# Moving the float32 remainders of the PEER stages from GpSimd to VectorE, and pinning the row gathers

## The chip, the cores and the metric

The kernel runs on 1 core of one Trainium2 chip. The metric is the device time in microseconds of one launch; a figure is the median of several runs. A profiled execution has a time of its own, which stands beside its span in the table below.

## What is computed

The reference is a two-block network on 512 tokens of width 1024: a first block (differential attention and a mixture of 16 experts), then a second block (forgetting attention, an RWKV-7 time mix, a gated merge, a layer norm) that ends in a PEER layer. Only the PEER layer and the last layer norm matter here:

```
q = (xb @ w_q).reshape(t, 8, 2, 128)                    # 8 heads, two halves each
s = einsum('thpd,hpkd->thpk', q, sub_keys)
top_s, top_i = top_k(s, 16)                             # per half
cand = top_s[.., 0, :, None] + top_s[.., 1, None, :]    # 16 x 16 sums
best_s, best_pos = top_k(cand, 16); idx = the pair's index in 16384 experts
gate = softmax(best_s)
h = gelu(einsum('thkd,td->thk', u_table[idx], xb))
y = einsum('thk,thkd->td', gate * h, v_table[idx])
```

## The kernel before

It is one program for one core, written in a framework that traces it and then fixes, at build time, the order of the instructions in each engine's queue: among the instructions whose inputs its own cost estimates call ready, the one that was traced first goes first. On the chip each queue then runs strictly in that order. `keep_in_program_order` pins one instruction behind the instruction that was traced just before it on the same engine; nothing else is pinned by it, and instructions traced later may still be placed ahead.

Matrix products of full float32 precision are made of three passes (`mm3`, lines 47 to 51). For that each operand is split in two halves by `split` (lines 53 to 61): ScalarE writes the rounded half `hi` (line 57), and VectorE, or the engine given as `eng`, writes the remainder `lo = src - hi` (line 58). `load_split` (lines 66 to 72) puts a load on SyncE's DMA queue in front of it.

The PEER layer (`peer`, from line 1747) works on 512 tokens in 4 tiles of 128. For the first three tiles (384 tokens) it is dense: all 16384 rows of the table u are multiplied with the tokens, in 128 blocks of 128 rows, and all rows of v are summed with weights that are zero except for the chosen ones. For the last tile the chosen rows alone are gathered (`peer_rows`, lines 1714 to 1744). The stages, with their time from the start of the span:

- **Top-k stage** (about 1268 to 1537 us). For each of 8 heads, `peer_topk` (line 1625) loads and splits the two query weights of the head (line 1631), multiplies, scores, and picks the 16 best on VectorE. After each head, `spill` (line 1779) multiplies the next 3, 4 or 5 blocks of u (`u_block`, line 1769: load, split, 24 matmuls into one of two PSUM banks, Gelu on ScalarE) and stores them in DRAM (`hd`), to use TensorE while VectorE sorts: 30 blocks in all.
- **Scatter stage** (about 1537 to 1707 us). `peer_scatter` (line 1691) is called 48 times. Each call makes one-hot tiles on VectorE (lines 1699, 1700, 1704: four instructions of 128x1024 float16), multiplies them on TensorE (line 1710) and copies the result to `Gs` (line 1712), from where 6 stores bring it to DRAM. After every second call one block of u is spilled: 24 blocks. I call two calls and one block a step.
- **Main loop** (from about 1707 us; 130 turns). It first spills 6 more blocks of u (line 1826), then for each of the 128 blocks loads the stored product or makes it, multiplies with `G`, splits it, loads and splits a block of v, and multiplies into six PSUM accumulators. Among these turns the 257 steps of `peer_rows` are dealt out: 128 times a gather of a row of u for each of 128 tokens (line 1725, a DMA of 128 x 4 KB issued by GpSimd, indices in SBUF) and a dot product with the token on VectorE (line 1732, pinned); one step for the weights; 128 times a gather of v and a multiply-add on VectorE (line 1741, pinned). The gathered rows have 5 buffers.

In the top-k and the scatter stage the splits of u (line 58 by `u_block`) and all query weights but the first have `eng` set to GpSimd. In the 6 blocks after the scatter stage and in the main loop VectorE makes them. GpSimd's other work here is two small tables (lines 1797, 1802), the two loads of the layer norm's rows at the start of the main loop (line 77, called by line 1836), the gathers, and four additions at the very end (line 1558).

Of the kernel before, what the change touches and what calls it, by code (L numbers as in the profile page):

```python
# [20 lines left out]
T, D, NT, KC = 512, 1024, 4, 8  # L21
# [6 lines left out]
class Kern:  # L28
# [1596 lines left out]
    def peer_topk(self, wp, h, xT, sk, iota16, pk):  # L1625

        nc, I = self.nc, self.I
        tv = self.t(wp, [128, 2, NT, 16], F32, "tv")
        ti = self.t(wp, [128, 2, NT, 16], U32, "ti")
        for s in range(2):  # L1630
            w = self.load_split(wp, I["wq"][2 * h + s], [128, KC, 128], "w", 2, 2, nc.gpsimd if h or s else None)
            p = self.psx()
            for kc in range(KC):
                self.mm3(p, [z[:, kc, :] for z in w], [z[:, kc, :] for z in xT], kc == 0, kc == KC - 1)
            q = self.t(wp, [128, T], F32, "q")
            nc.scalar.activation(q, p, AF.Copy)
            p = self.psx([128, NT, 128])
            for t in range(NT):
                nc.tensor.matmul(p[:, t, :], q[:, t * 128:(t + 1) * 128], sk[:, 2 * h + s, :], start=True, stop=True)
            sc = self.t(wp, [128, NT, 128], F32, "sc")  # L1640
            nc.scalar.activation(sc, p, AF.Copy)
            for t in range(NT):
                self.top16(wp, sc[:, t, :], 128, tv[:, s, t, :], ti[:, s, t, :], "t")

        cand = self.t(wp, [128, NT, 80], F32, "cand")
        nc.vector.tensor_tensor(cand[:, :, 0:16], tv[:, 0, :, 0:1].to_broadcast([128, NT, 16]), tv[:, 1], OP.add)
        nc.vector.tensor_tensor(cand[:, :, 16:72].rearrange("p t (a b) -> p t a b", b=8),
                                tv[:, 0, :, 1:8, None].to_broadcast([128, NT, 7, 8]),
                                tv[:, 1, :, None, 0:8].to_broadcast([128, NT, 7, 8]), OP.add)
        nc.vector.tensor_tensor(cand[:, :, 72:80], tv[:, 0, :, 8:16], tv[:, 1, :, 0:1].to_broadcast([128, NT, 8]), OP.add)  # L1650
        bs = self.t(wp, [128, NT, 16], F32, "bs")
        bp = self.t(wp, [128, NT, 16], U32, "bp")
        for t in range(NT):
            self.top16(wp, cand[:, t], 80, bs[:, t, :], bp[:, t, :], "c")

        pf = self.t(wp, [128, 2, NT, 16], F32, "pf")
        q, r = pf[:, 0], pf[:, 1]
        ai = self.t(wp, [128, NT, 16], I32, "ai")
        ab = self.t(wp, [128, 2, NT * 16], BF, "ab")
        a, b = (ab[:, i].rearrange("p (t k) -> p t k", t=NT) for i in range(2))  # L1660
        t9 = self.t(wp, [128, NT, 16], F32, "t9")
        nc.vector.tensor_copy(r, bp)
        nc.vector.tensor_scalar(ai, r, -3.5, 1.0 / 8, OP.add, OP.mult)
        nc.vector.tensor_copy(q, ai)
        nc.vector.scalar_tensor_tensor(r, q, -8.0, r, OP.mult, OP.add)
        nc.vector.scalar_tensor_tensor(t9, q, 9.0, r, OP.is_equal, OP.mult)
        nc.vector.tensor_tensor(r, r, t9, OP.subtract)
        nc.vector.scalar_tensor_tensor(a, q, -1.0, t9, OP.add, OP.add)
        nc.vector.tensor_scalar(a, a, 0.0, None, OP.max)
        nc.vector.tensor_scalar(t9, q, 1.0, 8.0, OP.is_equal, OP.mult)  # L1670
        nc.vector.tensor_tensor(b, r, t9, OP.add)
        tf = self.t(wp, [128, 2, NT, 16], BF, "tf")
        nc.vector.tensor_copy(tf, ti)
        for s in range(2):
            eq = self.t(wp, [128, 16, NT * 16], BF, "eq")
            nc.vector.tensor_tensor(eq, iota16, ab[:, s, None, :].to_broadcast([128, 16, NT * 16]), OP.is_equal)
            e4 = eq.rearrange("p a (t k) -> p t a k", t=NT)
            nc.vector.tensor_tensor(e4, e4, tf[:, s, :, :, None].to_broadcast([128, NT, 16, 16]), OP.mult)
            for n in (8, 4, 2):
                nc.vector.tensor_tensor(eq[:, 0:n], eq[:, 0:n], eq[:, n:2 * n], OP.add)  # L1680
            e1 = [eq[:, i].rearrange("p (t k) -> p t k", t=NT) for i in range(2)]
            nc.vector.tensor_tensor(pk[:, :, s, h, :], e1[0], e1[1], OP.add)
        g = pk[:, :, 2, h, :]
        nc.vector.tensor_tensor(g, bs, bs[:, :, 0:1].to_broadcast([128, NT, 16]), OP.subtract)
        nc.scalar.activation(g, g, AF.Exp)
        zs = self.t(wp, [128, NT], F32, "zs")
        nc.vector.tensor_reduce(zs, g, AX.X, OP.add)
        nc.vector.reciprocal(zs, zs)
        nc.vector.tensor_tensor(g, g, zs[:, :, None].to_broadcast([128, NT, 16]), OP.mult)
# [24 lines left out]
    def peer_rows(self, sp, x, pk):  # L1714


        nc, I = self.nc, self.I
        t, keep = NT - 1, self.tc.keep_in_program_order
        ix = self.t(sp, [128, 8, 16], U32, "ix")
        g = self.t(sp, [128, 8, 16], F32, "rg")  # L1720
        dots = self.t(sp, [128, 8, 16], F32, "dots")

        def row(name, h, j):
            r = self.t(sp, [128, D], F32, "row", 5)
            nc.gpsimd.indirect_dma_start(r, None, I[name], bass.IndirectOffsetOnAxis(ap=ix[:, h, j:j + 1], axis=0))  # L1725
            return r

        def dot(h, j):
            if j == 0:
                nc.vector.scalar_tensor_tensor(ix[:, h], pk[:, t, 0, h], 128.0, pk[:, t, 1, h], OP.mult, OP.add)  # L1730
            r = row("u", h, j)
            keep(nc.vector.tensor_tensor_reduce(r, r, x[:, t, :], 1.0, 0.0, OP.mult, OP.add, dots[:, h, j:j + 1]))  # L1732

        def weights():
            nc.scalar.activation(g, dots, AF.Gelu)
            nc.vector.tensor_tensor(g, g, pk[:, t, 2], OP.mult)
            nc.scalar.activation(x[:, t, :], x[:, t, :], AF.Copy, scale=2.0 ** 0.25)

        def add(h, j):
            r = row("v", h, j)  # L1740
            keep(nc.vector.scalar_tensor_tensor(x[:, t, :], r, g[:, h, j:j + 1], x[:, t, :], OP.mult, OP.add))  # L1741

        picks = [(h, j) for h in range(8) for j in range(16)]
        return [lambda a=a: dot(*a) for a in picks] + [weights] + [lambda a=a: add(*a) for a in picks]


    def peer(self, x):

        nc, I, tc = self.nc, self.I, self.tc
        NB, ND = 60, NT - 1  # L1750
        TD = ND * 128
        with ExitStack() as ph:
# [26 lines left out]
            def spill(n, eng=None):  # L1779
                for b in range(self.ahead, min(self.ahead + n, NB)):  # L1780
                    a = self.t(up, [128, TD], F32, "hs", 2)
                    u_block(b, a, eng)
                    nc.sync.dma_start(hd[b], a)
                self.ahead = min(self.ahead + n, NB)
# [9 lines left out]
            with ExitStack() as sub:  # L1794
# [3 lines left out]
                with tc.tile_pool(name="ptk", bufs=2) as wp, tc.tile_pool(name="psk", bufs=1) as kp:  # L1798
                    sk = self.t(kp, [128, 16, 128], F32, "sk")
                    nc.sync.dma_start(sk, I["sk"])  # L1800
                    iota16 = self.t(kp, [128, 16, NT * 16], BF, "iota16")
                    nc.gpsimd.iota(iota16, pattern=[[1, 16], [0, NT * 16]], base=0, channel_multiplier=0, allow_small_or_imprecise_dtypes=True)
                    for h in range(8):
                        self.peer_topk(wp, h, xT, sk, iota16, pk)
                        spill(5 if h == 7 else 4 - h % 2, nc.gpsimd)
                with tc.tile_pool(name="pgs", bufs=2) as wp:
                    keys = []
                    for t in range(ND):
# [9 lines left out]
                    for t in range(ND):  # L1818
                        for i in range(2):
                            Gs = self.t(wp, [128, 128, 64], F32, "Gs")  # L1820
                            for b in range(8):
                                self.peer_scatter(wp, *keys[t], i * 8 + b, Gs, iota2)
                                if b % 2 == 1:
                                    spill(1, nc.gpsimd)
                            nc.sync.dma_start(gd[2 * t + i], Gs)
            spill(NB)
            pss.close()
# [2 lines left out]
            wp = ph.enter_context(tc.tile_pool(name="pdw", bufs=2))  # L1830
# [167 lines left out]
```

## Time and profile before

| | |
|---|---|
| Runs | 2598.91 us median of 3 (2596.53 to 2601.98) |
| Profiled execution | 2601.8 us |
| its span, first to last instruction | 2600.1 us |
| granted TensorE clock, mean | 0.967 |
| TensorE busy (matmul) | 2411.4 us, 93% |
| VectorE busy | 1997.3 us, 77% |
| ScalarE busy | 1129.0 us, 43% |
| GpSimd busy | 941.2 us, 36% |

In the rows below PE is TensorE, DVE is VectorE, ACT is ScalarE, POOL is GpSimd and SP is SyncE. A group has the line, the engine and operation, output<-inputs, shapes and count, then busy time in us and the mean of one in ns, then the idle time of the engine just before it and what ended that. L58 is line 58 of the kernel. PEclk is the clock that TensorE was granted as a share of full speed: 1.00 is the level of 2.4 GHz, 0.50 that of 1.2 GHz.

### The profile page before, as it was taken

What the parts mean: (1) busy time and instruction counts of PE and PEld (TensorE: products, weight loads), DVE (VectorE), ACT (ScalarE), POOL (GpSimd) and SP (SyncE); (2) the same over time, 40 slices, a digit from 0 to 9 for tenths busy, and PEclk for the clock granted to TensorE, in tenths of its full rate; (3) what the DMA queues carried; (4) which work ended last, traced back from release to release, by engine and by line L of the source; (5) the groups of instructions that cost most, each with busy time, mean ns of one, the idle gap of its engine ahead of it and who ended that gap; (6) DMA issues with size and microseconds to landing.
All of it is one profiled execution on the core that took longest, in us unless ns stands there. A gap on an engine that the chain in (4) does not pass through costs nothing.

```text
span 2600.1 us, 36041 instructions
## 1 busy us (share of the span) xinstructions
PE 2411.4 (93%) x13302; PEld 1987.8 (76%) x13302; DVE 1997.3 (77%) x3696; ACT 1129.0 (43%) x1660; POOL 941.2 (36%) x674
## 2 busy tenths in 40 slices
PE   6999979999799999899989988899999999999998
PEld 5666666666577787777779878898788879888886
DVE  7698678988866558647699997857788778787886
ACT  3366546777544543224334434443333333332333
POOL 2577422223311103000255456614454434444440
PEclk8999989999899999899999999999999999999999
DMA  7442359999631122115254226689899899999992
GB/s 251 131 153 97 109 198 338 366 358 364 225 110 49 64 70 76 58 58 174 100 165 140 98 78 241 251 325 350 314 352 352 304 335 330 332 324 334 334 321 81
DMA packets 229671, 566.30 MB, mean 218 GB/s; under 512 B 27794, under 2 KB 83138, under 8 KB 228596
## 3 DMA queue, kind: packets, MB, share of 16 engines
q1 hardware_dynamic: 180512, 394.88, 43.4%
q0 software_dynamic: 44176, 159.38, 17.7%
q10 hardware_dynamic: 4804, 9.72, 1.0%
q8 instruction: 105, 1.72, 0.3%
q14 instruction: 74, 0.61, 0.1%
HBM read 511.99 MB, written 51.92 MB: 217 GB/s over the span
## 4 chain that ended last, share of the span: by engine, by line
PE 19%; DVE 12%; issue 12%; POOL 7%; DMA 6%; ACT 1%; SPq 0%; POOLq 0%; DVEq 0%; ACTq 0%
POOL row L1725 5%; PE psu L51 2%; PE psu L49 2%; DMA act<-hd 2%; PE psu L50 2%; DMA row<-in_v,ix 2%; POOL u_lo L58 2%; PE py L50 2%; PE py L51 2%; PE py L49 2%; DVE x L1741 1%; DMA row<-in_u,ix 1%; DVE ohB L1704 1%; PE psb L49 1%; PE psx L1710 1%
## 5 line engine op out<-in xcount | busy, mean ns | idle before, releaser
L51 PE MATMUL psu<-x4T_hi,u_lo 128*128 128x384 f32 x1024 | 347.5, 340 | 18.5 <-POOL u_lo L58 18.5
L49 PE MATMUL psu<-x4T_hi,u_hi 128*128 128x384 f32 x1024 | 350.0, 342 | 0.5 <-ACT act L1775 0.4
L50 PE MATMUL psu<-x4T_lo,u_hi 128*128 128x384 f32 x1024 | 346.5, 338 | 0.0
L50 PE MATMUL py<-v_lo,W_hi 128*128 128x512 f32 x768 | 304.7, 397 | 15.1 <-DVE v_lo L58 15.1
L49 PE MATMUL py<-v_hi,W_hi 128*128 128x512 f32 x768 | 304.1, 396 | 10.9 <-ACT W_hi L57 7.8
L51 PE MATMUL py<-v_hi,W_lo 128*128 128x512 f32 x768 | 304.3, 396 | 1.8 <-DVE W_lo L58 1.8
L1725 POOL DMA_INDIRECT row<-in_v,ix x128 | 185.7, 1450 | 224.4 <-DVE x L1741 192.9
L1725 POOL DMA_INDIRECT row<-in_u,ix x128 | 182.9, 1429 | 228.9 <-DVE dots L1732 203.6
L58 POOL TENSOR_TENSOR u_lo<-u_raw,u_hi 128x1024 fp32r<-128x1024 f32 x54 | 193.7, 3594 | 143.7 <-ACT u_hi L57 143.7
L57 ACT ACTIVATE W_hi<-act 128x384 fp32r<-128x384 f32 x128 | 66.5, 524 | 407.3 <-DVE act L1859 407.3
L58 DVE TENSOR_TENSOR ew_lo<-ew_raw,ew_hi 128x2048 fp32r<-128x2048 f32 x93 | 216.8, 2331 | 34.1 <-ACT ew_hi L57 32.8
L57 ACT ACTIVATE u_hi<-u_raw 128x1024 fp32r<-128x1024 f32 x128 | 134.8, 1055 | 188.3 <-PE psu L50 106.8
L51 PEld LDWEIGHTS psu<-x4T_hi,u_lo 128*128 128x128 f32 x1024 | 195.1, 191 | 19.5 <-POOL u_lo L58 19.4
L49 PEld LDWEIGHTS psu<-x4T_hi,u_hi 128*128 128x128 f32 x1024 | 195.4, 191 | 4.6 <-ACT act L1775 0.8
L50 PEld LDWEIGHTS psu<-x4T_lo,u_hi 128*128 128x128 f32 x1024 | 195.2, 191 | 3.6
L57 ACT ACTIVATE w_hi<-w_raw 128x1024 fp32r<-128x1024 f32 (+1 forms) x103 | 101.8, 992 | 221.0 <-PE psb L50 99.2
L57 ACT ACTIVATE ew_hi<-ew_raw 128x2048 fp32r<-128x2048 f32 x93 | 178.2, 1916 | 42.3 <-PE psa L51 41.3
L50 PEld LDWEIGHTS py<-v_lo,W_hi 128*128 128x128 f32 x768 | 146.7, 191 | 47.9 <-DVE v_lo L58 19.9
L1732 DVE CUSTOM_DVE_ANT_0 row<-row,x 128x1024 f32<-128x1024 f32 x128 | 155.7, 1239 | 34.9 <-DMA row<-in_u,ix 34.8
L1741 DVE SCALAR_TENSOR_TENSOR x<-row,rg,x 128x1024 f32<-128x1024 f32 x128 | 164.0, 1282 | 23.5 <-DMA row<-in_v,ix 21.8
L58 DVE TENSOR_TENSOR v_lo<-v_raw,v_hi 128x1024 fp32r<-128x1024 f32 x128 | 156.3, 1221 | 31.0 <-ACT v_hi L57 30.9
L49 PEld LDWEIGHTS py<-v_hi,W_hi 128*128 128x128 f32 x768 | 146.8, 191 | 41.6 <-ACT W_hi L57 9.8
(667 smaller groups left out, 5862.1 us busy)
## 6 DMA issues: line engine op xcount, KB each, us to landing
u_raw<-in_uT SPq DMA_DIRECT2D x128, 512.0 KB
v_raw<-in_v SPq DMA_DIRECT2D x128, 512.0 KB
ew_raw<-in_wgate SPq DMA_DIRECT2D x32, 1024.0 KB
ew_raw<-in_wup SPq DMA_DIRECT2D x32, 1024.0 KB
ew_raw<-in_wdown SPq DMA_DIRECT2D x32, 1024.0 KB
gd<-Gs SPq DMA_DIRECT2D x6, 4096.0 KB
G<-gd SPq DMA_DIRECT2D x32, 768.0 KB
w_raw<-in_w2b SPq DMA_DIRECT2D x39, 512.0 KB
```

The source lines that it names most:

```text
L49: mm(out, L[0], R[0], start=start, stop=False)
L50: mm(out, L[0], R[1], start=False, stop=False)
L51: mm(out, L[1], R[0], start=False, stop=stop)
L57: nc.scalar.activation(hl[0], src, AF.Copy)
L58: (eng or nc.vector).tensor_tensor(hl[1], src, hl[0].bitcast(F32), OP.subtract)
L1704: nc.vector.tensor_tensor(B[i], oh, bc(gp[:, i]), OP.mult)
L1710: nc.tensor.matmul(p[:, u, :], A[j], B[i][j], start=i == 0, stop=i == 1)
L1725: nc.gpsimd.indirect_dma_start(r, None, I[name], bass.IndirectOffsetOnAxis(ap=ix[:, h, j:j + 1], axis=0))
L1732: keep(nc.vector.tensor_tensor_reduce(r, r, x[:, t, :], 1.0, 0.0, OP.mult, OP.add, dots[:, h, j:j + 1]))
L1741: keep(nc.vector.scalar_tensor_tensor(x[:, t, :], r, g[:, h, j:j + 1], x[:, t, :], OP.mult, OP.add))
```

## The change

The engine argument of the split goes away at three places, so that the remainders of all blocks of u and of all query weights are made by VectorE; and the gather of a row is pinned behind the instruction traced before it on GpSimd.

```diff
@@ peer_topk
-            w = self.load_split(wp, I["wq"][2 * h + s], [128, KC, 128], "w", 2, 2, nc.gpsimd if h or s else None)
+            w = self.load_split(wp, I["wq"][2 * h + s], [128, KC, 128], "w", 2, 2)
@@ peer_rows
-            nc.gpsimd.indirect_dma_start(r, None, I[name], bass.IndirectOffsetOnAxis(ap=ix[:, h, j:j + 1], axis=0))
+            keep(nc.gpsimd.indirect_dma_start(r, None, I[name], bass.IndirectOffsetOnAxis(ap=ix[:, h, j:j + 1], axis=0)))
@@ peer
-                        spill(5 if h == 7 else 4 - h % 2, nc.gpsimd)
+                        spill(5 if h == 7 else 4 - h % 2)
...
-                                    spill(1, nc.gpsimd)
+                                    spill(1)
```

The instruction traced before the first gather on GpSimd is the second of the two row loads of line 1836; before each later gather it is the gather before.

## Rows read from the trace of the kernel before

**Rows 1.** Busy time by stage: stretch, its length, PE, PEld, DVE, ACT, POOL, PEclk, DMA share, GB/s

```profile
1268.00:1537.00 269.00, 247.61 (x1300) 226.44 (x1301) 248.52 (x1057) 110.06 (x148) 132.31 (x57) 0.96 0.42 140
1353.00:1529.00 176.00, 168.34 (x897) 154.50 (x896) 172.66 (x772) 72.09 (x96) 83.64 (x33) 0.98 0.37 121
1537.00:1707.00 170.00, 148.73 (x1303) 140.87 (x1303) 140.26 (x187) 80.73 (x142) 110.01 (x21) 0.94 0.59 219
1707.00:1748.00 41.00, 40.51 (x232) 39.73 (x231) 14.25 (x16) 15.80 (x22) 1.15 (x2) 1.00 0.94 340
1748.00:2560.00 812.00, 784.19 (x3735) 685.71 (x3734) 648.48 (x825) 277.86 (x382) 359.46 (x248) 0.98 0.91 326
```

**Rows 2.** Groups by line and shape, VectorE, 1280 to 1537 us

```profile
L1676 DVE TENSOR_TENSOR eq<-iota,ab 128x1024 bf16<-128x1024 bf16 x16 | 26.3, 1646 | 0.0
...
L1680 DVE TENSOR_TENSOR eq<-eq 128x512 bf16<-128x512 bf16 x16 | 19.8, 1235 | 0.0
...
L1647 DVE TENSOR_TENSOR cand<-tv 128x224 f32<-128x224 f32 x8 | 8.9, 1119 | 0.0
...
L1732 DVE CUSTOM_DVE_ANT_0 row<-row,x 128x1024 f32<-128x1024 f32 x3 | 5.9, 1974 | 1.0 <-DMA row<-in_u,ix 1.0
```

**Rows 3.** The same lines alone: shortest/median/longest in ns, first and last start

```profile
L1647 DVE TENSOR_TENSOR cand<-tv x8: 381/384/2895, 1306.0 to 1510.3; 128x224 f32<-128x224 f32 x8
L1676 DVE TENSOR_TENSOR eq<-iota,ab x16: 678/694/2897, 1315.0 to 1523.5; 128x1024 bf16<-128x1024 bf16 x16
```

**Rows 4.** Timeline of VectorE, 1522 to 1530 us: start, duration, instruction

```profile
1524.08 0.41 DVE L1680 TENSOR_TENSOR eq<-eq 128x512 bf16<-128x512 bf16 x1
```

**Rows 5.** Groups by line and shape, GpSimd, 1268 to 1537 us

```profile
L58 POOL TENSOR_TENSOR u_lo<-u_raw,u_hi 128x1024 fp32r<-128x1024 f32 x33 | 83.7, 2541 | 84.9 <-ACT u_hi L57 84.9
L58 POOL TENSOR_TENSOR w_lo<-w_raw,w_hi 128x1024 fp32r<-128x1024 f32 x15 | 39.1, 2605 | 35.7 <-ACT w_hi L57 35.7
L1725 POOL DMA_INDIRECT row<-in_u,ix x8 | 9.1, 1132 | 5.8 <-DVE pk L1689 3.9 <-issue 1.7 <-DVE tv L1619 0.2
```

**Rows 6.** Timeline of GpSimd and of ScalarE in the top-k stage

```profile
1323.14 1.05 POOL L1725 DMA_INDIRECT row<-in_u,ix  x1 [3.93 <-DVE pk L1689]
...
1346.57 0.26 ACT L1685 ACTIVATE pk<-pk 128x64 f32<-128x64 f32 x1 [12.65 <-DVE pk L1684]
```

**Rows 7.** Waits of TensorE, 1268 to 1537 us: total, times, longest

```profile
PE psx L1639 <- ACT q L1636: 10.5, 2, 8.6
```

**Rows 8.** Busy time in stretches of 5 us (columns as in rows 1)

```profile
1345.00:1350.00 5.00, 0.00 (x0) 0.00 (x0) 4.73 (x24) 3.40 (x5) 0.35 (x1) 0.64 0.11 39
1350.00:1355.00 5.00, 3.95 (x13) 3.53 (x14) 5.00 (x3) 1.60 (x3) 5.00 (x2) 0.50 0.31 101
```

**Rows 9.** Waits of TensorE, 1537 to 1760 us

```profile
PE psu L51 <- POOL u_lo L58: 18.5, 3, 6.4
```

**Rows 10.** The chain of work that ended last, 1241 to 1760 us: start, duration, what

```profile
1544.47 14.90 POOL u_lo L58
...
1599.78 14.31 POOL u_lo L58
...
1685.52 1.86 PE psx L1710 x32
1691.60 1.86 PE psx L1710 x32
```

**Rows 11.** Timeline of VectorE: two one-hot instructions in a row; two remainders in a row

```profile
1597.95 0.68 DVE L1700 TENSOR_TENSOR ohA<-iota,pkT 128x1024 f16<-128x1024 f16 x1
1598.55 0.68 DVE L1704 TENSOR_TENSOR ohB<-oh,gp 128x1024 f16<-128x1024 f16 x1
...
1754.43 2.35 DVE L58 TENSOR_TENSOR u_lo<-u_raw,u_hi 128x1024 fp32r<-128x1024 f32 x2
```

**Rows 12.** Timeline of GpSimd at the start of the main loop

```profile
1721.62 0.59 POOL L77 DMA_DIRECT2D lng<-in_ln_g  x1 [26.07 <-DVE lneps L1838]
...
1748.34 1.74 POOL L1725 DMA_INDIRECT row<-in_u,ix  x1 [25.57 <-DVE dots L1732]
```

## The prediction

> **What bounds the kernel now.** I read the busy time by stage first. The change touches the top-k stage (269 us), the scatter stage (170 us) and the first turns of the main loop [rows 1]. In the stretch from 1353 to 1529 us VectorE is busy for 172.7 of 176 us: the top-k stage is bound by VectorE, with TensorE close behind at 168.3 [rows 1]. The scatter stage is bound by nothing steadily: TensorE 148.7 and VectorE 140.3 of 170 us, at a granted clock of 0.94 [rows 1]. The main loop belongs to TensorE (784 of 812 us), with the DMA engines at a share of 0.91 [rows 1]. So GpSimd, which the change empties, is the bound nowhere; the question is what its instructions do to the others.
>
> Next the groups of VectorE, beside the shortest and median of the same lines. A one-hot compare of line 1676 takes 694 ns in the median but 1646 in the mean, and 2897 at its longest [rows 2, 3]. The 2.2 us between median and longest are nearly one whole remainder on GpSimd (mean 2541 and 2605 ns [rows 5]). The reader is to see that VectorE stands still behind GpSimd's instruction, now and then, in the stage in which VectorE is the bound.
>
> Then the chain of work in the scatter stage: it runs through remainders of u on GpSimd that took 14.9 and 14.3 us [rows 10], and TensorE waits three times, 18.5 us in all, for such a one [rows 9]. Here it is GpSimd that stands still, behind a run of VectorE instructions that start 0.60 us apart [rows 11].
>
> Last the hoisted row work. Eight gathers and three dot products run inside the top-k stage, from 1323 us on [rows 2, 5, 6], though they are traced in the main loop. The dots hold VectorE for 5.9 us and 1.0 us of waiting for data [rows 2]; after them ScalarE, stuck at an Exp, waits 12.65 us for VectorE [rows 6], and TensorE waits 8.6 us in turn [rows 7] and restarts at half clock [rows 8].
>
> **The change part by part, the top-k stage.** It removes 48 remainders from GpSimd (33 of u, 15 of w [rows 5]) and adds 48 to VectorE. Two in a row took 2.35 us on VectorE [rows 11], 1.18 each; 48 x 1.18 = 56.6 us. Those ahead of the first head fall where VectorE has most of its 20.5 us of idle time [rows 1]; I put six there, which leaves 42 x 1.18 = 49.6 us on the bound.
>
> What VectorE gets back are its stops. Counted from mean less undisturbed time: line 1676, 16 x (1646 - 694) = 15.2 us; line 1680 of 512 columns, 16 x (1235 - 410) = 13.2 us; line 1647, 8 x (1119 - 384) = 5.9 us [rows 2, 3, 4]. That is 34.3 us that are certain. At most each of the 48 costs 2.2 us, 106 us. I take 46, nearer the counted end, since the other lines with two inputs are few or short. The dots leave this stage too: 6.9 us. Net on VectorE: +49.6 - 46 - 6.9 = **-3.3 us**; with the counted stops alone +8.4, and at the other end no more than about -20, since TensorE needs 247.6 us of the 269 as it is [rows 1]. TensorE loses its wait of 8.6 us and its slow restart, but VectorE is the later of the two, so I credit only 2 us for that: **-5 us**.
>
> The Trainium skill, page "SBUF — State Buffer", section "Who interferes with whom", says that a VectorE instruction with two SBUF inputs and a GpSimd instruction that reads SBUF exclude each other, each holding a shared port for the whole instruction. By that alone a remainder on GpSimd would lose at most one VectorE instruction, 0.7 us, and be done in about 3.3 us; the scatter stage would have no stall and the change would gain nothing there (the sum below would be near -2). The measured 14.3 us say that the loser can lose many times in a row; the rows decide.
>
> **The scatter stage.** A step (two calls and one block) takes TensorE 6.08 us where nothing stalls: the starts of the scatter matmuls of neighbouring steps are 1685.52 and 1691.60 [rows 10]. On VectorE it will need 8 x 0.60 + 1.18 = 5.98 us [rows 11], with no stop behind GpSimd. So 24 steps are 24 x 6.08 = 146 us, against 170 now: at most 24 us, of which 18.5 are the named wait and the rest its slow restarts (a mean clock of 0.94 [rows 1]). With VectorE only 2% shorter than TensorE some steps will slip; I take **-19 us**, with 0 and -24 as ends.
>
> **The gathers.** Pinned behind the load of the layer norm's rows, which is issued at 1721.6 us [rows 12], the first gather can no longer go at 1323 us [rows 6]. Five go at once after that load, three more as dots end; now the ninth gather goes at 1748.3 [rows 12]. On GpSimd that costs nothing: it is idle then. The three dots, 3 x 1.2 us, go to a stretch where VectorE is busy for 14.3 of 41 us [rows 1]. But eight gathers are 8 x 512 KB = 4.2 MB, and they leave a stage with a DMA share of 0.42 for one with 0.91 to 0.94; at 326 GB/s [rows 1] that is 12.9 us of transfers, in front of loads of u and v on which the first turns depend. The share leaves some 7% free, and TensorE has the six spilled blocks in hand; I take **+3 us**, with 0 and +13 as ends. Within the loop the order of gathers was the order of the pinned dots already; the rest of the pins I cost at nothing: a gather waits for a buffer that a dot frees, as now [rows 12]. If gathers were placed later than now, the dots would come late, and with them the loads behind VectorE; that cover is VectorE's 160 us of idle time in the loop [rows 1].
>
> **Sum:** -5 - 19 + 3 = -21 us. The profiled execution took 2601.8 us, 2.9 more than the median of 2598.9; from the median, -21 gives 2578, from the profiled one 2581. I say **2579 us**.
>
> **The rivals.**
>
> *VectorE's queue takes over the waits (slower).* On GpSimd the remainders waited 84.9 + 35.7 = 120.6 us for ScalarE's halves, and nobody stood behind them but other remainders [rows 5]. On VectorE the sort, the scores' consumers and the Exp's input stand behind them. If a third of these waits is kept, 40 us come on top of a bound engine: -21 + 40 = +19, **2618 us**. It decides from 21 us on, a little over a sixth of the waits, 2.6 us a head. For it: VectorE is full at 98% [rows 1], so any wait there is a loss, and a remainder that comes late behind a sort starves TensorE, which then restarts at half clock [rows 8]. Against it: the order is built on the readiness of inputs, GpSimd's stops that it could not foresee are gone, and in the main loop VectorE makes such remainders with TensorE busy for 784 of 812 us [rows 1].
>
> *The scatter stage stays stuck.* If VectorE, at 5.98 of 6.08 us a step, falls behind, half the gain goes: **2589 us**.
>
> *The loop pays in full for the gathers.* +13 in place of +3: **2589 us**. For it: the DMA share of 0.94 just then [rows 1].
>
> *The pin does not bind.* If the dots stay hoisted, VectorE keeps 6.9 us, the loop gets 3 back: **2583 us**.
>
> *The stops were more than counted.* At the end that TensorE sets, -20 in the top-k stage: **2564 us**.
>
> **How the numbers follow.** The forecast, 2566 to 2588, gets 0.50; the pin that does not bind 0.05; the stuck scatter stage and the full price of the gathers, 2588 to 2593, 0.11 together; more stops, 2556 to 2566, 0.08; two of the bad cases together, or a small loss in VectorE's queue, which end within 0.2% of now (2593.7 to 2604.1; about what a measurement of this kernel can tell from no change), 0.09; the slower rival 0.17. So faster 0.74, same 0.09, slower 0.17. A range from 2560 to 2606 leaves out some of the upper gain and most of the slower rival, about 0.2. The forecast's own range, of one sign, is 2566 to 2588.
>
> **What would show it.** Right: no line 58 on GpSimd; longest of lines 1676 and 1647 near their medians; the scatter stage near 150 us with no wait of TensorE for `u_lo` over 2 us, at a clock near 1.00; no gather before the layer norm's rows; the Exp's longest wait on ScalarE well under 12 us. Wrong: waits of VectorE for `u_hi` or `w_hi` in the top-k stage beyond 20 us, the stage longer than 269 us with TensorE waiting for `u_lo` from VectorE, or waits for loads of u and v in the first turns of the loop.

## The result, and the profile after

The changed kernel takes **2560.36 us** (median of 4 runs, 2556.33 to 2562.07) against 2600.44 (4 runs, 2596.53 to 2603.17) beside it: a ratio of 0.9845, 95% interval 0.9826 to 0.9863. That is 40 us faster, where 21 us were forecast. 2560.36 lies inside the stated range of 2560 to 2606 us by 0.4 us, and below the forecast's own range of 2566 to 2588.

The profiled execution has a span of 2557.9 us against 2600.1. To see where the 42.2 us went, I take for each kernel the same marks: the start of the first transpose of line 1766, the first one of line 1811, the first and the last copy of line 1712, and the first and last multiplication with G of line 1859. The lines of one view, of the changed kernel (shortest/median/longest in ns, first and last start):

```profile
L1766 PE MATMUL psx<-ident,x x32: 272/273/476, 1272.0 to 1281.7; 128*128 128x128 f32 x32
...
L1811 PE MATMUL psx<-ident,pk x9: 272/273/329, 1512.7 to 1515.2; 128*128 128x128 f32 x9
...
L1712 ACT ACTIVATE Gs<-psx x96: 589/600/624, 1521.0 to 1661.4; 128x512 f32<-128x512 f32 x96
...
L1859 DVE TENSOR_TENSOR act<-act,G x128: 546/551/562, 1707.5 to 2534.1; 128x384 f32<-128x384 f32 x128
```

The same of the kernel before:

```profile
L1766 PE MATMUL psx<-ident,x x32: 272/273/472, 1268.0 to 1279.2; 128*128 128x128 f32 x32
...
L1811 PE MATMUL psx<-ident,pk x9: 421/421/478, 1528.8 to 1530.9; 128*128 128x128 f32 x9
...
L1712 ACT ACTIVATE Gs<-psx x96: 587/598/633, 1538.1 to 1706.5; 128x512 f32<-128x512 f32 x96
...
L1859 DVE TENSOR_TENSOR act<-act,G x128: 546/552/577, 1744.8 to 2575.9; 128x384 f32<-128x384 f32 x128
```

The differences of neighbouring marks, in us, for these two and for the experiments below (their names are explained there; "ahead" is the work before the PEER layer, which no kernel here touches but e12_all_vector):

| kernel | ahead | top-k | gap | scatter | loop's start | loop | end | top-k to end |
|---|---|---|---|---|---|---|---|---|
| before | 1268.0 | 260.8 | 9.3 | 168.4 | 38.3 | 831.1 | 24.2 | 1332.1 |
| after | 1272.0 | 240.7 | 8.3 | 140.4 | 46.1 | 826.6 | 23.8 | 1285.9 |
| after_again | 1272.6 | 241.2 | 8.3 | 140.5 | 45.7 | 823.4 | 23.8 | 1282.9 |
| e1_no_pin | 1269.6 | 243.3 | 8.3 | 141.3 | 38.8 | 827.1 | 23.8 | 1282.6 |
| e2_pin_only | 1268.7 | 254.0 | 9.1 | 169.6 | 45.5 | 828.0 | 24.2 | 1330.4 |
| e3_scatter_only | 1279.2 | 254.2 | 7.7 | 140.6 | 36.8 | 825.5 | 23.8 | 1288.6 |
| e4_topk_only | 1264.2 | 250.0 | 9.6 | 169.5 | 36.6 | 828.8 | 23.9 | 1318.4 |
| e5_early_gathers | 1268.7 | 241.0 | 8.3 | 140.5 | 36.7 | 826.2 | 23.8 | 1276.5 |
| e7_idle_subtract | 1273.4 | 294.8 | 7.0 | 140.5 | 46.5 | 829.3 | 23.8 | 1341.9 |
| e8_write_only | 1271.5 | 242.8 | 8.2 | 140.5 | 46.2 | 825.4 | 23.8 | 1286.9 |
| e9_w_back | 1266.3 | 242.3 | 8.3 | 141.5 | 46.1 | 824.7 | 23.8 | 1286.7 |
| e10_u_back | 1269.1 | 250.7 | 7.6 | 140.6 | 45.9 | 827.9 | 23.8 | 1296.5 |
| e11_half_subtract | 1273.7 | 258.9 | 7.0 | 140.5 | 46.8 | 828.6 | 23.8 | 1305.6 |
| e12_all_vector | 1273.1 | 241.1 | 8.3 | 140.5 | 45.6 | 823.7 | 23.8 | 1283.0 |

So the 42.2 us are +4.0 ahead of the change (where profiles of equal code differ by up to 15 us, so this is no effect of it), **-20.1 in the top-k stage**, -1.0 in the gap, **-28.0 in the scatter stage**, **+7.8 at the loop's start**, -4.5 in the loop and -0.4 at the end. The -4.5 has no cause that is shown here: the same code gave 826.6 and 823.4 us. Stages are compared below, not spans, since the stretch ahead of them varies so much.

Busy time by stage after, to be read beside [rows 1] (columns as there):

```profile
1272.00:1512.70 240.70, 236.09 (x1264) 215.39 (x1264) 230.94 (x1074) 108.71 (x146) 0.84 (x1) 0.99 0.41 131
1353.00:1510.00 157.00, 157.00 (x850) 144.96 (x850) 155.53 (x762) 69.55 (x92) 0.00 (x0) 1.00 0.38 121
1521.00:1662.00 141.00, 139.19 (x1291) 133.83 (x1289) 139.78 (x212) 79.48 (x140) 0.00 (x0) 1.00 0.70 265
1662.00:1703.00 41.00, 36.72 (x201) 36.08 (x200) 13.30 (x15) 11.52 (x16) 11.05 (x10) 0.96 0.98 388
```

Same view, the top-k stage of before between its own marks:

```profile
1268.00:1528.80 260.80, 239.46 (x1264) 218.82 (x1264) 240.94 (x1035) 109.82 (x147) 132.31 (x57) 0.96 0.43 143
```

In the top-k stage TensorE stood idle for 260.8 - 239.5 = 21.3 us; now it is 4.6 us, and from 1353 to 1510 us it is busy without a gap at full clock. The bound has moved from VectorE to TensorE. The groups of VectorE there (1272 to 1521 us), to be read beside [rows 2]:

```profile
L58 DVE TENSOR_TENSOR u_lo<-u_raw,u_hi 128x1024 fp32r<-128x1024 f32 x32 | 38.9, 1214 | 1.0 <-ACT u_hi L57 1.0
...
L58 DVE TENSOR_TENSOR w_lo<-w_raw,w_hi 128x1024 fp32r<-128x1024 f32 x16 | 19.4, 1212 | 4.3 <-ACT w_hi L57 4.3
...
L1676 DVE TENSOR_TENSOR eq<-iota,ab 128x1024 bf16<-128x1024 bf16 x16 | 11.0, 687 | 0.0
...
L1680 DVE TENSOR_TENSOR eq<-eq 128x512 bf16<-128x512 bf16 x16 | 6.7, 416 | 0.0
...
L1647 DVE TENSOR_TENSOR cand<-tv 128x224 f32<-128x224 f32 x8 | 3.0, 378 | 0.0
```

The remainders take 1.21 us each, near the 1.18 taken from [rows 11], and the means of the other three lines have fallen to their undisturbed values; for ScalarE's halves VectorE waits 4.3 + 1.0 = 5.3 us in all. The longest of line 1676, 2897 ns in [rows 3], is now 693. Of the waits, those that answer to [rows 6, 7] are small too:

```profile
PE psx L1639 <- ACT q L1636: 1.1, 1, 1.1
...
DVE tv L1619 <- ACT sc L1641: 1.1, 1, 1.1
...
ACT pk L1685 <- DVE pk L1684: 27.3, 8, 4.1
```

Before, the first was 10.5 us, the second was 13.3 us in 4 waits, and the longest of the third was 12.65.

The chain of work that ended last, in the scatter stage, is now a train on TensorE in place of the two long remainders of [rows 10]:

```profile
1543.43 1.86 PE psx L1710 x32
...
1658.82 1.86 PE psx L1710 x32
```

From 1543.43 to 1658.82 there are 19 steps of 6.07 us in the mean, without a slip.

### The profile page after: what moved, and what is told of

Its sections match the earlier page's. It is cut to its first block, busy times and chain, and to the rows that moved or that the text cites. A ratio compares the mean times of both kernels' runs of the same rounds, so it can differ in the third digit from the quotient of the medians.

```text
span 2557.9 us, 36037 instructions
## 1 busy us (share of the span) xinstructions
PE 2396.9 (94%) x13302; PEld 1977.2 (77%) x13302; DVE 1991.3 (78%) x3765; ACT 1130.3 (44%) x1660; POOL 710.5 (28%) x605
## 4 chain that ended last, share of the span: by engine, by line
PE 18%; issue 16%; DVE 11%; POOL 8%; DMA 3%; ACT 1%; POOLq 0%; DVEq 0%; ACTq 0%
POOL row L1725 8%; PE psu L49 2%; PE psu L51 2%; PE psu L50 2%; DMA row<-in_v,ix 2%; PE psx L1710 2%; PE py L50 1%; PE py L51 1%; PE py L49 1%; DVE u_lo L58 1%; PE psb L49 1%; PE psb L50 1%; PE psb L51 1%; DVE eq L1678 1%; DVE x L1741 1%
## 5 line engine op out<-in xcount | busy, mean ns | idle before, releaser
L1732 DVE CUSTOM_DVE_ANT_0 row<-row,x 128x1024 f32<-128x1024 f32 x128 | 153.2, 1219 | 46.2 <-DMA row<-in_u,ix 46.2
L51 PEld LDWEIGHTS py<-v_hi,W_lo 128*128 128x128 f32 x768 | 146.1, 190 | 34.9 <-DVE W_lo L58 4.6
```

What stands on the lines that cost most here:

```text
L51: mm(out, L[1], R[0], start=False, stop=stop)
```

## The experiments

The theories. **Stops**: a GpSimd subtraction, which reads SBUF, holds up VectorE's next instruction for nearly its whole length; the top-k stage pays for that. **Lateness**: the stage pays because TensorE waits for remainders that GpSimd finishes late. Both could be true of different stages. A third question is what the pin of the gathers is worth.

### One part at a time (e1 to e4)

e1_no_pin is the change without the pin, e2_pin_only the pin alone:

```diff
# e1_no_pin, against after
-            keep(nc.gpsimd.indirect_dma_start(...))
+            nc.gpsimd.indirect_dma_start(...)
# e2_pin_only, against before
-            nc.gpsimd.indirect_dma_start(...)
+            keep(nc.gpsimd.indirect_dma_start(...))
```

> The change without its pin: all remainders on VectorE, gathers free to be placed early. Theory A (three separate causes: VectorE's stops behind GpSimd in the top-k stage, GpSimd's starving in the scatter stage, the hoisted dots): the dots are back in the top-k stage and cost about the 7 us that they held VectorE, the loop gets 3 back; scatter stage 141 us as with the change; in all 2564 to 2570 us, 4 to 10 above the change. Rival B (the hoisted dots are the main cause of the top-k stage's loss, by way of ScalarE's Exp and TensorE's restart): the top-k stage falls back by 12 us or more, 2572 to 2580 us.

> The pin alone: remainders stay on GpSimd. Theory A: top-k stage about 7 us shorter, scatter stage 169 us as before, loop 3 longer: about 2596 us. Rival B: top-k stage 15 us or more shorter, 2583 to 2588 us.

e3_scatter_only and e4_topk_only divide the moved remainders:

```diff
# e3_scatter_only, against before
-                                    spill(1, nc.gpsimd)
+                                    spill(1)
# e4_topk_only, against before
-            w = self.load_split(..., "w", 2, 2, nc.gpsimd if h or s else None)
+            w = self.load_split(..., "w", 2, 2)
...
-                        spill(5 if h == 7 else 4 - h % 2, nc.gpsimd)
+                        spill(5 if h == 7 else 4 - h % 2)
```

> Only the 24 blocks of the scatter stage have their remainders on VectorE. Theory A: scatter stage 169 to 141 us, all else as before: 2572 us, no longer wait of TensorE for u_lo, one-hot instructions at their median of 0.68 us throughout. Rival C (what the scatter stage gains is given back at the start of the loop, where the DMA share is 0.94): 2580 to 2590 us.

> Only the top-k stage has its remainders on VectorE; no pin. Theory A: that stage shorter by the stops less the remainders, some 12 of the 20 us that the whole change took from it (the dots keep theirs): about 2588 us; lines 1676 and 1647 at their medians throughout. Rival D (the waits for ScalarE's halves move into VectorE's queue once the dots disturb it): no gain or a loss, 2598 us or more.

Measured, as ratios to before on the same chip (2604.27 us, 23 runs): e1 0.9818 (0.9792 to 0.9844), e2 1.0008 (0.9992 to 1.0024), e3 0.9856 (0.9831 to 0.9882), e4 0.9954 (0.9935 to 0.9974). So the scatter stage's remainders carry most of the gain, the top-k stage's some 12 us, and the pin nothing that is clear of noise. The times expected for e1 and e2 were missed: leaving out the pin was to cost 4 to 10 us, and the pin alone to gain some 4. The top-k stage did what was expected of e2 (6.8 us shorter), but the loop's start took 7.2 back.

The table of stages says more. The scatter stage falls by 27 to 28 us in every kernel in which its own remainders are VectorE's (e1, e3, after) and in no other. The **top-k stage falls in three portions**: by 10.8 us when its own remainders move (260.8 to 250.0 in e4; also 254.2 to 243.3 from e3 to e1), by 6.6 us when only the scatter stage's move (260.8 to 254.2 in e3), and by another 2.6 us with the pin (243.3 to 240.7). The portions depend on the order: the pin alone, with the remainders still on GpSimd, takes 6.8 us from the stage (260.8 to 254.0 in e2), so that the three alone add up to 24.2 and not to 20.1.

The middle portion was a surprise: e3 changes no remainder of the top-k stage. But three blocks of the scatter stage are taken ahead, into the end of the top-k stage, where the last head's one-hot work still runs. GpSimd's timeline before has them, and VectorE's three instructions that take far longer than usual under them (0.18, 0.22 and 1.22 us each in the mean after):

```profile
1516.90 2.42 POOL L58 TENSOR_TENSOR u_lo<-u_raw,u_hi 128x1024 fp32r<-128x1024 f32 x1 [2.88 <-ACT u_hi L57]
1519.94 2.40 POOL L58 TENSOR_TENSOR u_lo<-u_raw,u_hi 128x1024 fp32r<-128x1024 f32 x1 [0.62 <-ACT u_hi L57]
1524.16 2.53 POOL L58 TENSOR_TENSOR u_lo<-u_raw,u_hi 128x1024 fp32r<-128x1024 f32 x1 [1.82 <-ACT u_hi L57]
```

```profile
1517.09 2.27 DVE L1669 TENSOR_SCALAR ab<-ab 128x64 bf16<-128x64 bf16 x1
...
1520.00 2.42 DVE L1671 TENSOR_TENSOR ab<-pf,t 128x64 bf16<-128x64 f32 x1
...
1524.42 3.36 DVE L1678 TENSOR_TENSOR eq<-eq,tf 128x1024 bf16<-128x1024 bf16 x1
```

Three stops of some 2.2 us are 6.6 us on the chain that ends the stage. In e4, where only these three are left, the waits of TensorE show the same sum at the transposes that open the scatter stage:

```profile
PE psx L1811 <- DVE pk L1682: 6.7, 1, 6.7
PE psx L1639 <- ACT q L1636: 2.6, 2, 1.5
```

The second line corrects the prediction in another place. I had put TensorE's wait of 8.6 us [rows 7] down to the hoisted dot products. In e4 the dots are still hoisted and the wait is down to 1.5 us; in e2 the dots are gone, the remainders are still GpSimd's, and its longest is 1.9 us; in e3, which has both, it is 8.5. In these runs the long wait came only with both together.

### GpSimd's reads, without their use (e7, e11) and its writes alone (e8)

In e7_idle_subtract VectorE makes every remainder, as after, and GpSimd subtracts once more, into a tile that nobody reads. By its groups these are 30 subtractions of u and 15 of w, 45 and not the 47 of my expectation. e11_half_subtract does half the columns of each.

```diff
@@ load_split, for the top-k stage's loads
         self.split(hl, raw, eng=eng)
+        if extra:
+            junk = self.t(extra, shape, F32, "junk", 1)
+            self.nc.gpsimd.tensor_tensor(junk, raw, hl[0].bitcast(F32), OP.subtract)
# e11_half_subtract: the same, with raw[:, 0:4, :] and hl[0][:, 0:4, :]
```

> The changed kernel, and in the top-k stage GpSimd does each subtraction of before once more into a tile that nobody reads: 47 subtractions of 2.2 us or more that read SBUF, while every remainder that TensorE uses still comes from VectorE. Theory one: before paid for VectorE being stopped by GpSimd's reads. Then the longest one-hot instructions of the top-k stage (L1676, L1678, L1680) are back at 2.5 to 3.5 us, these lines' sums are back near before's (26 us for L1676, 24 for L1678, 26 for L1680), the stage is 20 to 50 us longer than the changed kernel's 240.7 us, and TensorE waits more for what VectorE makes. Theory two: before paid for TensorE waiting for remainders that GpSimd finished late, the stops being hidden. Then the stage stays within 5 us of 240.7 us, since nothing waits for the added work.

> The kernel with GpSimd's 47 idle subtractions, each over half the columns (128x512 in place of 128x1024). If VectorE loses the time of the GpSimd instruction that holds it, the longest stopped instructions of the top-k stage fall from 2.4 us to 1.2 to 1.6 us and the stage is 20 to 32 us longer than the changed kernel's 241 us, in place of the 54 us of the full ones. If a stop has a price of its own that does not depend on the length, the longest stay above 2 us and the stage is 45 to 55 us longer.

In e8_write_only GpSimd writes zeros to each remainder tile, ahead of VectorE:

```diff
@@ load_split, for the top-k stage's loads
+        if extra:
+            self.nc.gpsimd.memset(hl[1].bitcast(F32), 0.0)
         self.split(hl, raw, eng=eng)
```

> The changed kernel, and in the top-k stage GpSimd fills each remainder tile with zeros before VectorE writes it: 47 GpSimd instructions that write SBUF and read none of it. If only a GpSimd instruction that reads SBUF keeps VectorE's two-input instructions out, the one-hot lines keep the changed kernel's longest (L1676 0.7 us or less) and the stage is within 5 us of 240.7 us (the fill can be early, since it waits only for the buffer). If any SBUF access by GpSimd does, the longest one-hot instructions grow by up to one fill and the stage by 10 us or more.

e7 makes the top-k stage **54.1 us longer** than after (294.8 against 240.7), more than the 20 to 50 expected, and every other stage stays within 3 us; with a ratio of 1.0052 (1.0028 to 1.0076) the kernel is a little slower than before, though no engine uses a result of the added work. Busy time of the stage in e7:

```profile
1273.40:1568.20 294.80, 250.16 (x1265) 225.54 (x1266) 290.26 (x1078) 108.51 (x145) 123.19 (x46) 0.93 0.33 107
```

VectorE is busy for 59.3 us more than after, with the same instructions, and full (290.3 of 294.8). ScalarE does wait for buffers that the added work still reads, 20.6 us in all, but about as long as it did before (21.9 us for remainders on GpSimd), and VectorE has no idle time that this could cause. So stops alone are enough to make the stage longer. That lateness is not needed, the kernel before shows itself: in its top-k stage TensorE waits for no remainder at all. Beside the wait for q of [rows 7], these are all of its named waits from 1268 to 1537 us:

```profile
PE psx L1811 <- DVE pk L1682: 5.7, 1, 5.7
PE psx L1766 <- DVE x L1558: 5.0, 2, 2.7
PE psx L1766 <- DVE x L1609: 0.8, 1, 0.8
```

With that the lateness theory falls for this stage. What I expected of the lines was wrong, though: L1676, L1678 and L1680 (three lines further down in e7) keep their undisturbed length, and others are hit. Timelines of both engines in e7:

```profile
1376.61 5.01 POOL L74 TENSOR_TENSOR junk<-w_raw,w_hi 128x1024 f32<-128x1024 f32 x2
...
1377.10 2.22 DVE L1650 TENSOR_TENSOR cand<-tv 128x224 f32<-128x224 f32 x1
...
1379.24 0.28 DVE L1625 MAX8 tv<-trest 128x8 f32<-128x128 f32 x1
...
1379.44 2.23 DVE L1653 TENSOR_TENSOR cand<-tv 128x32 f32<-128x32 f32 x1
```

The reader is to see that an addition of 128x32, 0.17 us undisturbed, takes 2.23 because it starts under a GpSimd subtraction, while a MAX8 between two stopped ones runs in its usual 0.28 us. Which line is hit depends on the moment, not on its size. At some 2.2 us each, 59.3 us would be 27 stops for 45 subtractions; that is an estimate, not a count.

With subtractions of half the size (median 1.32 us against 2.46) e11's stage is 18.2 us longer than after, VectorE's busy time 23.3 us (254.2 against 230.9), and the longest of the stopped additions is half as long too. The lines of e7 and of e11 (each the same two lines of code):

```profile
L1649 DVE TENSOR_TENSOR cand<-tv x8: 199/1191/2187, 1319.0 to 1554.8; 128x64 f32<-128x64 f32 x8
...
L1653 DVE TENSOR_TENSOR cand<-tv x8: 169/2222/2284, 1315.4 to 1551.1; 128x32 f32<-128x32 f32 x8
```

```profile
L1649 DVE TENSOR_TENSOR cand<-tv x8: 203/1064/1183, 1311.0 to 1518.2; 128x64 f32<-128x64 f32 x8
...
L1653 DVE TENSOR_TENSOR cand<-tv x8: 171/177/1111, 1309.5 to 1516.7; 128x32 f32<-128x32 f32 x8
```

A stop grows with GpSimd's instruction (the longest of L1653 is 2.1 us over its undisturbed 0.17 for subtractions of 2.46, and 0.9 for 1.32); no price of its own is to be seen. The stage's 18 us lie just under the 20 to 32 expected. In e11 and in e7 alike the stage grows by 5 us less than VectorE's busy time (18.2 against 23.3, 54.1 against 59.3); that fits the idle time that VectorE has after, where TensorE is the bound.

e8's stage is 242.8 us, within 2.1 of after, and no two-input line is hit, though in its timelines from 1300 to 1520 us 20 such instructions start while a fill runs. Four lines with one input were, though (L1671, L1672, L1675 and the cast of L1666 in e8's numbers): the sum of each has grown by 0.8 to 1.0 us, one stop by one zero fill of 0.95 us. Shortest/median/longest of two of them in e8, and of a two-input line:

```profile
L1671 DVE TENSOR_SCALAR ab<-ab x8: 173/181/1017, 1318.2 to 1508.9; 128x64 bf16<-128x64 bf16 x8
...
L1675 DVE CAST tf<-ti x8: 216/223/1009, 1310.6 to 1501.5; 128x128 bf16<-128x128 uint32 x8
...
L1652 DVE TENSOR_TENSOR cand<-tv x8: 167/172/177, 1309.0 to 1499.8; 128x32 f32<-128x32 f32 x8
```

The Trainium skill, page "SBUF — State Buffer", section "Who interferes with whom", draws this line: a VectorE instruction with two SBUF inputs contends with GpSimd instructions that read, not with ones that only write, while some one-input forms, scalar operations and casts among them, can take both of the shared ports. e7 and e8 agree with it, by the 2.23 and 1.02 us above.

### Which remainders (e9, e10)

```diff
# e9_w_back, against after
-            w = self.load_split(..., "w", 2, 2)
+            w = self.load_split(..., "w", 2, 2, nc.gpsimd if h or s else None)
# e10_u_back, against after
-                        spill(5 if h == 7 else 4 - h % 2)
+                        spill(5 if h == 7 else 4 - h % 2, nc.gpsimd)
```

> The changed kernel with only the 15 query-weight remainders of the top-k stage back on GpSimd (the 32 of the u blocks stay on VectorE). If before paid for stops, which every GpSimd subtraction can cause alike, the 15 of 47 carry their share of the 10.8 us that the whole move gave: the stage is 2 to 6 us longer than the changed kernel's 241 us. If before paid because TensorE waited for the query weights' late remainders (the waits for q, 10.5 us), nearly all of it comes back here: 8 to 12 us longer, with 8 us or more of waits for q.

> The changed kernel with only the 32 u-block remainders of the top-k stage back on GpSimd (the query weights' stay on VectorE). By stops: 32 of 47 subtractions, 5 to 10 us more than the changed kernel's 241 us, and the one-hot lines' longest back at 2.2 us or more. By late query weights: 0 to 3 us more, since u blocks have three buffers and nothing waits for them.

The query weights' 15 remainders cost 1.6 us when they go back (242.3; 2 to 6 were expected by stops), the u blocks' 30 cost **10.0 us** (250.7). In ratios: 0.9846 (0.9822 to 0.987) and 0.9869 (0.9842 to 0.9895); these two overlap, so the stages decide. Late query weights are out as the cause: in e9 TensorE waits for q for 1.6 us in all. In e10 the longest of line 1676 is back where it was before:

```profile
L1676 DVE TENSOR_TENSOR eq<-iota,ab x16: 685/693/2890, 1316.3 to 1516.0; 128x1024 bf16<-128x1024 bf16 x16
```

The sums behind this are instructive. By the groups, in e10 VectorE gives back 35.2 us of remainders and gets 36 us of stops; in e9 it is 18.2 us against 15.5. **By these sums the exchange is nearly even.** By busy time in the stage, which counts the overlap of neighbouring instructions once, VectorE works 236.5 us in e10 and 229.6 in e9, against 230.9 after: 5.5 of e10's 10.0 us are more work and the rest more idle time (14.2 against 9.8 us). Why the u blocks' stops cost so much more than the query weights' is not shown. That they stand on the chain from a head's sort to its result (L1646 to L1680) is not enough: 32.8 of e10's 36 us do, but so do 12.7 of e9's 15.5 (L1669, L1670 and L1680).

### The pin and the loop's start (after_again, e5)

> The changed kernel once more, beside the others of this call, for comparison on one chip. Expected: about 2560 us, a ratio of 0.982 to 0.986; top-k stage near 241 us, scatter stage near 140 us, 46 us from the scatter's last activation to the loop's first dW.

e5_early_gathers takes the pin away again and computes the row indices of head 0 ahead of the loop, so that gathers can go early while the dot products cannot:

```diff
# against after
-            keep(nc.gpsimd.indirect_dma_start(...))
+            nc.gpsimd.indirect_dma_start(...)
...
-            if j == 0:
+            if j == 0 and h:
...
+        def first():
+            nc.vector.scalar_tensor_tensor(ix[:, 0], pk[:, t, 0, 0], 128.0, pk[:, t, 1, 0], OP.mult, OP.add)
... # peer, traced after the scatter stage
+            first()
```

> The changed kernel with the gathers unpinned and only the row indices of head 0 computed ahead of the loop, so that five row gathers go out before the burst of loads that opens the loop while all dot products stay in the loop. If the loop's start pays the pinned gathers because they run in the middle of that burst (46.1 us from the scatter's last activation to the first dW, against 38.8 without the pin), that piece falls back to 39 to 41 us, the other stages stay within 3 us of the changed kernel's, and the time is 2 to 7 us under the changed kernel's, at or under the version without a pin. If instead it pays for the 16 dot products and index work moved into the loop's first turns, the piece stays at 45 to 47 us and the time equals the changed kernel's.

GpSimd's timeline after shows the first gathers pinned behind the layer norm's rows:

```profile
1677.44 0.56 POOL L77 DMA_DIRECT2D lng<-in_ln_g  x1 [404.61 <-DMA u_raw<-in_uT]
...
1678.85 1.04 POOL L1725 DMA_INDIRECT row<-in_u,ix  x1 [0.30 <-issue]
```

They run into a stretch with a DMA share of 0.98 (0.94 before, [rows 1]). VectorE waits for the first rows, and a remainder of u stands in its queue behind the dots. VectorE's timeline after, and a wait of TensorE from 1657 to 1703 us:

```profile
1689.39 1.23 DVE L1732 CUSTOM_DVE_ANT_0 row<-row,x 128x1024 f32<-128x1024 f32 x1 [8.22 <-DMA row<-in_u,ix]
...
1692.36 1.23 DVE L1732 CUSTOM_DVE_ANT_0 row<-row,x 128x1024 f32<-128x1024 f32 x1 [1.74 <-DMA row<-in_u,ix]
...
1693.51 1.22 DVE L58 TENSOR_TENSOR u_lo<-u_raw,u_hi 128x1024 fp32r<-128x1024 f32 x1
```

```profile
PE psu L51 <- DVE u_lo L58: 4.0, 1, 4.0
```

In e5 five gathers go between 1340.5 and 1346.9 us and all 128 dots stay in the loop (the first at 1692.9):

```profile
1340.51 1.04 POOL L1725 DMA_INDIRECT row<-in_u,ix  x1 [71.03 <-DVE ai L1663]
...
1346.92 0.94 POOL L1725 DMA_INDIRECT row<-in_u,ix  x1 [0.30 <-issue]
```

The loop's start falls from 46.1 to **36.7 us**, as short as in the kernels without a pin (36.6 to 38.8), with the other stages as after and with all dots in the loop. So the pin's price there was the transfers in the burst and not the dots. From the top-k stage on e5 is the shortest of all (1276.5 us against 1285.9 and 1282.9 for after). Its time, 2552.7 us or 0.9812 (0.9781 to 0.9843), stands beside 2558.9 or 0.982 (0.979 to 0.985) for after_again on the same chip: the intervals overlap, so that it beats the changed kernel is likely from the stages and not shown by the times. Against before it is clearly faster.

### The same lesson elsewhere (e12)

```diff
@@ split, against after
-            (eng or nc.vector).tensor_tensor(hl[1], src, hl[0].bitcast(F32), OP.subtract)
+            nc.vector.tensor_tensor(hl[1], src, hl[0].bitcast(F32), OP.subtract)
```

> The changed kernel with the last 12 weight remainders that GpSimd makes in earlier stages (4 at 25 to 56 us, 8 at 986 to 1034 us) on VectorE too. If GpSimd subtractions cost the same wherever VectorE has work, 12 x (2.2 - 1.2) = some 12 us at most, 3 to 8 us where half of them hit. If it pays only where VectorE is the bound or nearly (it is busy 58 to 77 of 100 us at 900 to 1100 us, TensorE 87 to 99), the time is within 2 us of the changed kernel's in the same call.

2549.66 us, 0.979 (0.9764 to 0.9816), against after's 0.982 (0.979 to 0.985) on another chip: by the ratios some 8 us less, with overlapping intervals, and the changed kernel was not run beside it. In the profile the start of the top-k stage, by which all of this edit's effect must show, is 1273.1 against 1272.0 and 1272.6, where equal code varies by 15 us. So neither 3 to 8 us nor nothing is shown.

## Why the prediction was right, and where its sizes were off

**Luck.** That the time lies in the stated range is in part luck. The forecast gave 0.50 to 2566 to 2588 us, and the result fell where it gave 0.08, to more stops. The two large terms were both too small, by 15 and 9 us, and the third hid 4 us of that. The same kernel's median on another chip (2558.87) would have been outside. The causes named were right; the sizes were not.

**What bounds.** Right that VectorE was stopped by GpSimd in the stage that it bounds, and that GpSimd was held up in the scatter stage. All of the signs listed as right came: no line 58 on GpSimd there, the longest of lines 1676 and 1647 at 693 and 385 ns, no long wait for `u_lo` in the scatter stage at a clock of 1.00, gathers after the layer norm's rows, Exp's longest wait 4.1 us. The scatter stage was announced near 150 us and took 141.

**Top-k stage, forecast -5, measured -20.** The step that failed is VectorE's net of -3.3 us, and with it "VectorE is the later of the two, so I credit only 2 us". Head 0's first sort divides the stage, as the prediction did with its six remainders. Ahead of it the six fell into idle time as put there (11.9 us of it before, 6.6 after), and that stretch got 1.8 us shorter (25.7 to 23.8). Behind it the time fell from 235.1 to 216.9 us: 13.5 us are VectorE's busy time (227.1 to 213.7), against the 3.3, and 4.8 its idle time (8.0 to 3.2), against the 2.

The busy time's terms, by the groups of that stretch: the stops are 48.9 us against 46 taken (eight groups of before less those of after: 15.3 + 13.1 + 5.9 + 4.3 + 3.9 + 2.2 + 2.1 + 2.1). The remainders are 39 and 47.2 us, against 42 and 49.6, since three of the 48 belong to blocks of the scatter stage. The dots are 6.1, against 5.9 of work in the forecast's 6.9. That makes -7.8. All groups together fall by 9.7 (283.0 to 273.3), so small ones add 1.9; the rest, near 4 us, is overlap of neighbouring instructions, which a sum of lengths counts twice and busy time once.

Of the idle time, these are VectorE's two longest waits for scores before:

```profile
1293.67 0.49 DVE L1619 MAX8 tv<-sc 128x8 f32<-128x128 f32 x2 [8.93 <-ACT sc L1641]
...
1301.76 0.49 DVE L1619 MAX8 tv<-sc 128x8 f32<-128x128 f32 x2 [3.05 <-ACT sc L1641]
```

Both stand in head 0 and make 12.0 of the 13.3 us. They are in e2 as well (8.75 and 3.04), and in e4, where only the top-k stage's remainders moved, 1.1 us are left: the moved remainders are work for a time in which VectorE had none. What removed the rest of the idle time is not traced. That three blocks of the scatter stage stop the last head (6.6 us) I had not seen at all. The ceiling that I named, about -20 because TensorE sets it, is where the stage ended.

**Scatter stage, forecast -19, measured -28.** The step of 6.08 us was right within a hundredth. Two sizes were off: I set 24 steps against the stage, where between the first and the last copy lie 140.4 / 6.08 = 23.1; so the ceiling was 168.4 - 140.4 = 28, not 24. And I took off 5 us because "with VectorE only 2% shorter than TensorE some steps will slip"; none did, with VectorE busy for 139.8 and TensorE for 139.2 of 141 us.

One reading was too small. The 14.90 and 14.31 us of [rows 10] are only the pieces of two remainders that lie on the chain. The instructions themselves took 21.46 and 20.94 us, and a third took 20.34. GpSimd's group over the whole kernel has the longest, and VectorE's timeline has what ended it:

```profile
L58 POOL TENSOR_TENSOR u_lo<-u_raw,u_hi x54: 2355/2478/21456, 1272.8 to 1692.6; 128x1024 fp32r<-128x1024 f32 x54
```

```profile
1556.48 0.68 DVE L1699 TENSOR_TENSOR oh<-iota,pkT 128x1024 f16<-128x1024 f16 x1
1563.92 0.69 DVE L1700 TENSOR_TENSOR ohA<-iota,pkT 128x1024 f16<-128x1024 f16 x1 [6.76 <-PE psx L1710]
```

VectorE's train of one-hot instructions ends at 1557.16 us, because the next one waits for TensorE, which waits for this very remainder; 2.2 us later, at 1559.36, the remainder is done. The other two end 2.2 us after VectorE's last one-hot as well. So GpSimd got through only when VectorE had run out of work. The prediction's other reckoning, by which a remainder would be done in some 3.3 us and the stage gain nothing, falls with this and with the 28 us.

**Gathers, forecast +3, measured +7.3** (38.8 without the pin in e1, 46.1 with it; 38.3 to 45.5 in e2). The mechanism was the one named, transfers ahead of loads in a stretch that is full; the end of +13 was the better guide. What I missed is the other side: the pin also takes dots out of the top-k stage, worth 2.6 us there (6.8 with the remainders on GpSimd, e2), so that the pin's net is some +5 by stages, and nothing that the times can show (0.9818 without it, 0.982 and 0.9845 with it).

**The rivals.** VectorE's queue did not take over the waits: of the 120.6 us that the remainders waited on GpSimd, 5.3 came back in the top-k stage (4.3 + 1.0), a quarter of the 21 us from which it decides. The scatter stage did not stay stuck. The pin did bind. The loop paid 7 us, not the full 13. The rival "the stops were more than counted" gave 2564 and was nearest, on its figure for the stage; its mechanism was the smaller part of it, since the stops were only 3 to 5 us more than taken.

## What to carry to other kernels

An instruction on an idle engine is not free if it can stop the engine that bounds the stage: look at the longest against the median of every short VectorE line, and count the ones that differ by one GpSimd instruction. Here the stops cost VectorE about as much time as doing the work there (36 against 35.2 us in e10). Look for idle time of the bound engine that moved work can fill, and for the next stage's work that was taken ahead. A pin that takes loads out of a slack stage into a full one has a price at that place, and issuing only the transfers early, with their consumers left where they are, avoided it.

## What was not expected of the hardware

- The stops go by the other engine's instruction and not by the victim's size: 0.17 us became 2.23, and halving GpSimd's instruction halved the longest (1.11 to 1.18 us). MAX8 ran through in 0.28 us.
- One-input scalar operations and casts were stopped even by a GpSimd instruction that only writes (0.18 to 1.02 us, under fills of 0.95), and two-input ones were not.
- The two sides do not lose alike. VectorE lost at most about one GpSimd instruction at a time (2.1 to 2.2 us), but three GpSimd remainders behind back-to-back VectorE instructions took 20.3 to 21.5 us, against 2.48 in the median, and ended 2.2 us after VectorE ran dry; with GpSimd out of the way the same VectorE train runs without a gap. The Trainium skill, page "SBUF — State Buffer", section "Who interferes with whom", lets the instruction that issues first hold the ports for its whole length, with the other blocked. That fits each single stop; that one side loses many times in a row it does not say.
